# A two-layer hybrid decoder step: short head sums, fp32r norm sums, ordered weight parts and gating in two lines

## The chip, the cores and the metric

The kernel runs on one core of one Trainium2 chip. The metric is the device time of one execution, in microseconds (us); lower is better. Engines are named as the profile does: PE is TensorE's matmul, PEld its weight load, DVE is VectorE, ACT is ScalarE, POOL is GpSimd, SP is SyncE, which issues most transfers.

## The reference

One inference step of two layers, for a prompt of 256 rows and 8 sample rows that share all weights; D = 1024, feed-forward width 2816, everything in f32.

```python
def rmsnorm(x, g):
    y = x * lax.rsqrt(jnp.mean(x * x, axis=-1, keepdims=True) + EPS)
    return y * g
...
for i in range(DEPTH):                                     # 2
    x = x + 0.5 * swiglu(rmsnorm(x, norm_ffn1[i]), ...)
    h = rmsnorm(x, norm_mix[i])
    if i % 2 == 0:
        y, buf = short_conv_mixer(h, ...)                  # gated convolution of width 3
    else:
        y, S = hgrn2_mixer(h, rec_state, ...)              # 8 heads of 128, gated linear recurrence
    x = x + y
    x = x + cross_attn(rmsnorm(x, norm_xattn[i]), mem_k[i], mem_v[i], ...)   # 256 memory rows, 4 heads
    x = x + 0.5 * swiglu(rmsnorm(x, norm_ffn2[i]), ...)
y = rmsnorm(x, norm_final)
```

In the recurrent mixer the output of each head is `q` applied to the state, for the samples `o = (q*f) @ S0 + (q.k) v`; then

```python
o = rmsnorm(o, g_onorm) * silu(g)      # a norm over the 128 columns of each head
y = o.reshape(B, T, D) @ w_out
```

## The kernel before

The activations stay in SBUF, turned: `xT` holds 8 blocks (KT) of 128 columns of x on 128 partitions, with 264 columns (NC = 256 prompt rows + 8 samples). The weights stream through once. Each weight half (512 rows by 256 columns) is loaded (`raw`), rounded to fp32r on ScalarE (`wh`, L106) and its remainder computed on VectorE, in some stages on GpSimd (`wl`, L118). The activations are split the same way (`xh`, `xl`, L325 and L327). A product is then three fp32r matmuls, `wh*xh`, `wh*xl` and `wl*xh` (`mm3`, L303 to L305). Some smaller products are plain f32 matmuls, which show as two records each in the trace.

`project` runs a stage's chunks of 256 output columns. The first two chunks run together, staggered, in 16 groups of 6 matmuls, and hold all four PSUM banks for matmuls (`mm_bank`); the others follow one at a time. After a chunk half, `evac` reads the bank. It is issued under a raised priority, so the tile scheduler may put it ahead of other work of that engine.

All else is woven into the matmuls by `flow`. A `tick` (every 12 matmuls or so) advances the weights by one half (a split of `wl`, a rounding of `wh`, a load) and then takes one step of the front generator of each of three lanes. A generator that ends is taken out at the next step, and the next one of its lane comes up. The order in which the program issues things is not quite that in which an engine runs them: the scheduler fixes an order per engine by priority and its own estimate of what is ready, and the engines then run that order.

What the change and the prediction's steps touch:

- `Norm`: each block's square is added up on GpSimd (`nacc`, L336). After the last block, `finish` (lane 2) waits three steps, sums over partitions with an f32 matmul with `ones_d` (1/D everywhere, L345), and turns this into R, the reciprocal root: logarithm and exponential on ScalarE (L283), a Newton step on VectorE (L294, L298, L299). R multiplies the first bank of the next stage (L680 in the feed-forward, L814 in the attention, L741 and L743 in the convolution, L1046 in the recurrence). The first norm of the first layer is made in `start` instead.
- `out_proj`: the output projection of a mixer or an attention; `evac` adds the bank to `xT` (L722) and hands the block to the next norm.
- `attention`: `mem_split` (lane 1) rounds and splits the memory rows into `mh` and `ml` (L805, L806), one block per step; `do_kv` reads them after the queries' projection.
- `rec`: 16 chunks in the order f, q, f, q, i, i for heads 0 to 3 (group a = 0), the same for heads 4 to 7 (a = 1), then four chunks g. `chain(a)` (lane 0) makes the score matrices, `outputs(a)` (lane 1) the prompt's head outputs, `samples(a)` (lane 1) the samples': 16 matmuls per pair of heads with 32 columns of `qfz`, the product q*f (`pqs`, L1223), one copy of 512 columns to `os`, four transposes (`pqt`, L1238) and four additions that pick the diagonal (L1247). `head_norms(a)` (lane 2) squares the heads, sums over each head's 128 partitions with four matmuls with `strip` (`pm`, L1262) so that head hh's sum lies on partitions 32hh to 32hh+31, and makes `rs`, the reciprocal root. `gated(p)` (lane 2) spreads one row of `rs` over 128 partitions by a matmul with a column of the identity (`prs`, L1281), multiplies (L1285, L1286) and splits the result for the output projection (`yh` in the buffers `kg`, L1287; `yl` in `qf`, L1288). `before(k)` steps the flow until head k is made.

Lane 2 holds, in this order, `head_norms(0)`, `head_norms(1)`, `gated(0)` to `gated(3)`.

## Time and profile before

| | us |
|---|---|
| median of three runs | 1312.07 |
| lowest and highest | 1311.18, 1312.28 |
| profiled execution | 1312.63 |
| its span, first to last instruction | 1310.5 |

The profile is of one execution. Beside the page, these views are used: the waits (who waited for whom), the timeline (instructions of an engine in order of time: start, duration, engine, line, operation, tiles out<-in, forms and xcount; in brackets the idle time before one and what ended it), and the groups of instructions by line. Matmuls are pipelined, so their durations overlap; their cost is read from the distance between starts.

| engine | busy us | share of the span |
|---|---|---|
| PE | 1288.9 | 98% |
| DVE | 822.4 | 63% |
| ACT | 689.4 | 53% |
| POOL | 292.3 | 22% |

### The profile page before, as it was taken

The numbers are of one execution on the slowest core, as the hardware profiler recorded it, in microseconds if no ns is written. First come the engines' busy times: TensorE is split into PE (matmuls) and PEld (weight loads), VectorE is DVE, ScalarE is ACT, GpSimd is POOL, SyncE is SP. The second block draws the span as 40 slices with busy tenths as digits, with TensorE's granted clock in tenths as the row PEclk, the third lists the DMA queues.
The fourth block names the chain that finished last, engine by engine and source line by source line (L and its number), as shares of the span: only waits on it lengthen the run. The fifth ranks groups of instructions, "written<-read, shape, count | busy, mean of one in ns | idle before, by whom it ended". The sixth has DMA issues, their size and how long they took to land.

```text
span 1310.5 us, 25974 instructions
## 1 busy us (share of the span) xinstructions
PE 1288.9 (98%) x10330; PEld 1244.2 (95%) x10330; DVE 822.4 (63%) x1570; ACT 689.4 (53%) x1125; POOL 292.3 (22%) x236
## 2 busy tenths in 40 slices
PE   8999999999999999999999999999999999999997
PEld 7999999999869999999999999999999778999996
DVE  6655567759826655556555445878699637766454
ACT  6454544445545645544545544655665446666442
POOL 3211231212741111132111132000013521211220
PEclk9999999999999999999999999999999999999998
DMA  8796555646997666556666656554448995776650
GB/s 281 223 296 183 165 179 177 208 140 201 360 374 214 192 181 180 178 173 189 188 179 181 180 177 187 155 177 149 152 143 255 390 336 148 226 214 203 200 171 34
DMA packets 263099, 266.75 MB, mean 204 GB/s; under 512 B 8697, under 2 KB 259577, under 8 KB 260930
## 3 DMA queue, kind: packets, MB, share of 16 engines
q1 hardware_dynamic: 257150, 259.78, 63.8%
q10 hardware_dynamic: 5828, 5.32, 1.2%
q8 instruction: 81, 1.33, 0.4%
q14 instruction: 40, 0.33, 0.1%
HBM read 255.00 MB, written 10.07 MB: 202 GB/s over the span
## 4 chain that ended last, share of the span: by engine, by line
PE 92%; DVE 4%; ACT 2%; issue 1%; DMA 1%; POOL 0%; DVEq 0%; SPq 0%; ACTq 0%; POOLq 0%
PE pj L303 19%; PE pj L304 19%; PE pj L305 19%; PE dn L303 7%; PE dn L305 7%; PE dn L304 6%; PE kv L828 2%; PE kv L830 2%; PE kv L829 2%; DVE wl L118 1%; PE spv L984 1%; DVE xl L327 1%; PE psc L910 1%; PE pl L1139 1%; PE pj L370 1%; ACT wh L106 1%
## 5 line engine op out<-in xcount | busy, mean ns | idle before, releaser
L118 DVE TENSOR_TENSOR wl<-raw,wh 128x1024 fp32r<-128x1024 f32 (+1 forms) x347 | 425.4, 1230 | 247.4 <-ACT wh L106 232.3
L303 PE MATMUL pj<-xh,wh 128*128 128x264 f32 x1952 | 560.6, 287 | 2.0 <-DVE xT L722 2.0
L304 PE MATMUL pj<-xl,wh 128*128 128x264 f32 x1952 | 553.6, 284 | 0.0
L305 PE MATMUL pj<-xh,wl 128*128 128x264 f32 x1952 | 552.8, 283 | 0.0
L106 ACT CAST wh<-raw 128x1024 fp32r<-128x1024 f32 (+1 forms) x406 | 415.0, 1032 | 247.5 <-PE pj L304 123.7
L303 PEld LDWEIGHTS pj<-xh,wh 128*128 128x128 f32 x1952 | 367.7, 188 | 4.1 <-DVE xT L722 2.9
L304 PEld LDWEIGHTS pj<-xl,wh 128*128 128x128 f32 x1952 | 367.9, 189 | 0.3
L305 PEld LDWEIGHTS pj<-xh,wl 128*128 128x128 f32 x1952 | 366.2, 188 | 0.0
L303 PE MATMUL dn<-ah,wh 128*128 128x264 f32 x704 | 200.9, 285 | 0.0
L305 PE MATMUL dn<-ah,wl 128*128 128x264 f32 x704 | 200.0, 284 | 0.0
L304 PE MATMUL dn<-al,wh 128*128 128x264 f32 x704 | 199.4, 283 | 0.0
L118 POOL TENSOR_TENSOR wl<-raw,wh 128x1024 fp32r<-128x1024 f32 (+1 forms) x61 | 142.9, 2351 | 193.6 <-ACT wh L106 127.4
L688 POOL TENSOR_TENSOR al<-a,ah 128x264 fp32r<-128x264 f32 x88 | 90.2, 1027 | 418.3 <-ACT ah L687 418.2
L305 PEld LDWEIGHTS dn<-ah,wl 128*128 128x128 f32 x704 | 132.7, 188 | 0.0
L303 PEld LDWEIGHTS dn<-ah,wh 128*128 128x128 f32 x704 | 132.4, 188 | 0.2
L304 PEld LDWEIGHTS dn<-al,wh 128*128 128x128 f32 x704 | 132.5, 188 | 0.0
L283 ACT ACTIVATE g<-g 128x264 f32<-128x264 f32 x88 | 37.0, 424 | 81.3 <-DVE g L680 80.9
L687 ACT CAST ah<-a 128x264 fp32r<-128x264 f32 x88 | 36.0, 413 | 64.9 <-DVE a L686 64.4
L325 ACT ACTIVATE xh<-xT,gains 128x264 fp32r<-128x264 f32 x56 | 28.8, 514 | 77.2 <-DVE xT L714 59.2
L882 DVE CUSTOM_DVE_ANT_0 junk<-ring,pq 128x256 f32<-128x256 f32 x128 | 53.6, 419 | 3.7
L686 DVE TENSOR_TENSOR a<-g,pj 128x264 f32<-128x264 f32 x88 | 37.1, 426 | 28.7 <-PE pj L305 28.6
L680 DVE TENSOR_TENSOR g<-pj,R_norm_ffn 128x264 f32<-128x264 f32 x88 | 37.5, 429 | 27.4 <-PE pj L305 27.2
(321 smaller groups left out, 1497.8 us busy)
## 6 DMA issues: line engine op xcount, KB each, us to landing
raw<-in_w_ffn_gate_dram SPq DMA_DIRECT2D x88, 512.0 KB, 4.8
raw<-in_w_ffn_up_dram SPq DMA_DIRECT2D x88, 512.0 KB, 4.1
raw<-in_w_ffn_down_dram SPq DMA_DIRECT2D x64, 512.0 KB, 3.6
ring<-in_cache_mem_k_dram SPq DMA_DIRECT2D x16, 1024.0 KB, 8.5
raw<-in_w_xkv_dram SPq DMA_DIRECT2D x64, 256.0 KB, 3.8
ring<-in_cache_mem_v_dram SPq DMA_DIRECT2D x16, 1024.0 KB
raw<-in_w_rec_in_dram SPq DMA_DIRECT2D x32, 512.0 KB, 5.3
raw<-in_w_ffn_down_dram SPq DMA_DIRECT2D x32, 384.0 KB, 3.1
```

Source lines behind the costliest of these rows:

```text
L106: self.pin(copy(wh[:, :n], self.raw[i][:, :n]))
L118: self.pin(eng.tensor_sub(wl[:, :n], self.raw.pop(i)[:, :n], wh[:, :n].bitcast(F32)))
L283: in_line(nc.scalar.activation(dst, src, func, **kw))
L303: nc.tensor.matmul(ps, wh[:, s], rh, start=first, stop=False)
L304: nc.tensor.matmul(ps, wh[:, s], rl, start=False, stop=False)
L305: nc.tensor.matmul(ps, wl[:, s], rh, start=False, stop=last)
L325: pin(nc.scalar.activation(h, src, AF.Copy, scale=g))
L680: nc.vector.tensor_mul(g, ps, norm.R)
L686: nc.vector.tensor_mul(a, g, ps)
L687: nc.scalar.copy(ah[:, blk], a)
L688: nc.gpsimd.tensor_sub(al[:, blk], a, ah[:, blk].bitcast(F32))
L882: nc.vector.tensor_tensor_reduce(junk, t[:, i % 8], pq[:, :XD], 1.0, 0.0, ALU.mult, ALU.add, sc[:, h, i : i + 1])
```

## The change

1. Norm sums: `nacc` is split into a rounded part (ScalarE) and the remainder (VectorE) in the step in which the sum used to be issued, and two steps later two fp32r matmuls with an fp32r `ones_d` replace the f32 one. In steps: three waits, the split, two waits, the matmuls.
2. Head sums: four matmuls with a `mean` of 32 columns, each into its own 32 partitions, replace four accumulating ones with 128 columns.
3. `rs` is made fp32r: a copy rounds it, and one VectorE step leaves the rounded value on every partition but 1, 33, 65 and 97, where the remainder is kept (`seconds_of` is -1 there and 0 elsewhere). `pairs` adds a head's two rows in one fp32r matmul.
4. Samples: `qfz` holds the products on a diagonal of 4 by 4 for each half of the samples, so that matmuls with 4 columns accumulate a whole half of a head on 4 partitions; four strips for the four halves of a pair, four narrow copies, one transpose, one addition.
5. `gated(0)` and `gated(1)` go to lane 0; `made` becomes a set.
6. `mem_split` starts six steps later.
7. Weight parts: after the last sum of `out_proj` is issued and until the first two chunks of the next stage are, each `wl` on VectorE gets an ordering dependency (no semaphore) on that sum.

```diff
@@ Weights._split
-        self.pin(eng.tensor_sub(wl[:, :n], self.raw.pop(i)[:, :n], wh[:, :n].bitcast(F32)))
+        ins = eng.tensor_sub(wl[:, :n], self.raw.pop(i)[:, :n], wh[:, :n].bitcast(F32))
+        self.pin(ins)
+        if eng is nc.vector:
+            self.behind(ins)
@@ trunk_step
+    def order(ins, first, reason):
+        info = mybir.DependencyInfo(mybir.DependencyClass.NoSync, mybir.DependencyReason.DATA)
+        tc.add_manual_dep(ins.ins, first.name, info, reason=reason)
@@ Norm.finish
             yield
             yield
             yield
+            hi, lo = (cp.tile([P, NC], F32R, tag="nsq", name=n, bufs=2) for n in ("nhi", "nlo"))
+            nc.scalar.copy(hi, self.acc)
+            nc.vector.tensor_sub(lo, self.acc, hi.bitcast(F32))
+            yield
+            yield
             ps = aux_bank("ps_ms")
-            nc.tensor.matmul(ps[:, :NC], ones_d, self.acc, start=True, stop=True)
+            nc.tensor.matmul(ps[:, :NC], ones_d, hi, start=True, stop=False)
+            nc.tensor.matmul(ps[:, :NC], ones_d, lo, start=False, stop=True)
@@ project, after the first two chunks
             W.release()
+            W.behind = lambda ins: None
@@ prepare
+        nc.vector.tensor_add(pairs, ident[:, ::32], ident[:, 1::32])
+        nc.vector.reduce_sum(seconds_of, ident[:, 1::32], axis=AX.X)
+        nc.vector.tensor_scalar(seconds_of, seconds_of, -1.0, None, op0=ALU.mult)
@@ out_proj
-            nc.vector.tensor_add(xT[:, k], xT[:, k], ps)
+            add = nc.vector.tensor_add(xT[:, k], xT[:, k], ps)
+            if k == KT - 1:
+                W.behind = lambda ins: order(ins, add.ins, "the sum that frees a bank")
@@ attention, mem_split
+                for _ in range(6):
+                    yield
@@ rec
-            qfz = rp.tile([P, RH, 32], F32, name="qfz")
+            qfz = rp.tile([P, RH, 2, 16], F32, name="qfz")
+            os = rp.tile([P, P], F32, name="os")
+            nc.gpsimd.memset(os, 0.0)
...
-            nc.gpsimd.memset(strip[:, 3 * 32 : 4 * 32], 1.0 / P)
+            mean = rp.tile([P, 32], F32, name="mean")
+            nc.gpsimd.memset(mean, 1.0 / P)
@@ evac of a g chunk
                     if j == 1:
-                        flow.spawn(2, gated(p))
+                        flow.spawn(2 * a, gated(p))
@@ samples
-                    for hh in range(2):
-                        for hf in range(2):
-                            for j in range(4):
-                                nc.tensor.matmul(
-                                    ps[32 * j : 32 * j + 32, (2 * hh + hf) * P : (2 * hh + hf + 1) * P],
-                                    qfz[:, 2 * p + hh],
-                                    S0[:, hh, 4 * hf + j],
-                                    start=True,
-                                    stop=True,
-                                )
+                    for j in range(4):
+                        for c in range(4):
+                            hh, hf = divmod(c, 2)
+                            nc.tensor.matmul(
+                                ps[32 * c : 32 * c + 4, :P],
+                                qfz[:, 2 * p + hh, hf, 4 * j : 4 * j + 4],
+                                S0[:, hh, 4 * hf + j],
+                                start=j == 0,
+                                stop=j == 3,
+                            )
...
-                    os = tl("os", 1, (P, 4 * P))
-                    nc.scalar.copy(os, ps)
+                    for c in range(4):
+                        nc.scalar.copy(os[32 * c : 32 * c + 4], ps[32 * c : 32 * c + 4, :P])
...
-                    for i in range(4):
-                        nc.tensor.transpose(pt[:, i * P : i * P + P], os[:, i * P : i * P + P], ident)
+                    nc.tensor.transpose(pt[:, :P], os, ident)
@@ head_norms
-                    at = 32 * (GH - 1 - hh)
-                    nc.tensor.matmul(pm[:, :NC], strip[:, at : at + P], s["f"][:, hh], start=hh == 0, stop=hh == GH - 1)
+                    nc.tensor.matmul(pm[32 * hh : 32 * hh + 32, :NC], mean, s["f"][:, hh], start=True, stop=True)
...
-                newton(rs, pm[:, :NC], tmp)
+                newton(rr, pm[:, :NC], tmp)
+                nc.scalar.copy(rs, rr)
+                nc.vector.scalar_tensor_tensor(rs, rs.bitcast(F32), seconds_of, rr, op0=ALU.mult, op1=ALU.add)
@@ gated
-                        pr, ident[:, 32 * hh : 32 * hh + 1].broadcast_to([P, P]), s["rs"], start=True, stop=True
+                        pr, pairs[:, hh : hh + 1].broadcast_to([P, P]), s["rs"], start=True, stop=True
...
-                    made[0] = h + 1
+                    made.add(h)
@@ before
-                while made[0] <= k:
+                while k not in made:
```

## The prediction

> **What bounds the kernel now.** I read the page first: the busy shares, the granted clock and the chain that ended last.

> ```profile
> span 1310.5 us, 25974 instructions
> ...
> PE 1288.9 (98%) x10330; PEld 1244.2 (95%) x10330; DVE 822.4 (63%) x1570; ACT 689.4 (53%) x1125; POOL 292.3 (22%) x236
> ...
> PEclk9999999999999999999999999999999999999998
> ...
> PE 92%; DVE 4%; ACT 2%; issue 1%; DMA 1%; POOL 0%; DVEq 0%; SPq 0%; ACTq 0%; POOLq 0%
> ```

> TensorE is busy for 98% of the span at full clock, and 92% of the chain is its own. So a microsecond of matmul work taken out anywhere is a microsecond off the end, unless a wait grows into its place. The few per cent that belong to VectorE (DVE) are places where TensorE (PE) stands still. The view of waits, of PE alone, names those that the change can touch:

> ```profile
> PE pj L303 <- DVE xT L722: 2.0, 4, 1.0
> ...
> PE pj L303 <- ACT kg L1287: 0.3, 1, 0.3
> ```

> L722 is the sum in `out_proj` that frees a PSUM bank; it holds PE up four times (two mixers, two attentions). `kg` is the first gated head, under the buffer name that it reuses. I then went through PE's timeline around each operation that the diff rewrites, because durations of matmuls overlap: what a matmul costs is the distance between the starts of its neighbours.

> **The norm sums (ones_d).** A sum of the second layer's first norm, in PE's timeline:

> ```profile
> 624.08 0.28 PE L304 MATMUL pj<-xl,wh 128*128 128x264 f32 x1
> 624.20 0.28 PE L305 MATMUL pj<-xh,wl 128*128 128x264 f32 x1
> 624.32 0.61 PE L345 MATMUL ps_ms<-nacc_norm_ffn,ones_d 128*128 128x264 f32 x2
> 624.57 0.48 PE L303 MATMUL pj<-xh,wh 128*128 128x264 f32 x1
> 624.89 0.29 PE L304 MATMUL pj<-xl,wh 128*128 128x264 f32 x1
> ```

> An fp32r matmul over 264 columns starts 0.12 after its neighbour. The f32 sum is two passes (x2): from 624.20 to 624.89 is 0.69; less the two fp32r matmuls in it (0.24) it costs 0.45. The change puts two fp32r matmuls there, 0.24. Seven norms go through `finish` (the first of the eight does not): 7 x 0.21 = 1.5 us gained.

> **Spreading the head norms (prs).** In the same view, at the end of the recurrent layer's projection:

> ```profile
> 947.38 0.28 PE L305 MATMUL pj<-xh,wl 128*128 128x264 f32 x1
> 947.50 0.61 PE L1281 MATMUL prs<-rs,ident 128*128 128x264 f32 x2
> 947.75 0.48 PE L303 MATMUL pj<-xh,wh 128*128 128x264 f32 x1
> 948.06 0.28 PE L304 MATMUL pj<-xl,wh 128*128 128x264 f32 x1
> ```

> From 947.38 to 948.06 is 0.68, less 0.24: 0.44. After the change the rounded value and its remainder lie on two partitions of `rs`, and one fp32r matmul with `pairs` adds them: 0.12. Eight heads: 8 x 0.32 = 2.6 us.

> **The head norms' sums (pm).** Four f32 matmuls into one accumulator become four with 32 columns each, into four separate strips of the array:

> ```profile
> 944.15 0.28 PE L305 MATMUL pj<-xh,wl 128*128 128x264 f32 x1
> 944.27 1.94 PE L1262 MATMUL pm<-f,strip 128*128 128x264 f32 x8
> 945.85 0.48 PE L303 MATMUL pj<-xh,wh 128*128 128x264 f32 x1
> 946.17 0.28 PE L304 MATMUL pj<-xl,wh 128*128 128x264 f32 x1
> ```

> Now they take 2.02 less 0.24, 1.78. The nearest row for the new form is `pqs`, which already uses four strips:

> ```profile
> 853.48 0.28 PE L305 MATMUL pj<-xh,wl 128*128 128x264 f32 x1
> 853.69 1.08 PE L1223 MATMUL pqs<-ring,qfz 128*32 128x128 f32 x32
> 854.70 0.39 PE L303 MATMUL pj<-xh,wh 128*128 128x264 f32 x1
> 854.93 0.28 PE L304 MATMUL pj<-xl,wh 128*128 128x264 f32 x1
> ```

> Its 32 passes take 1.45 less 0.24, 1.21. One pass over 128 columns is 0.11 (the transposes below), so 32 passes four abreast are 0.88, and 0.33 goes into entering and leaving the strips. For `pm`: 8 passes four abreast are two of 0.22, 0.44, and with 0.33 that is 0.77. Gain 2 x (1.78 - 0.77) = 2.0 us. The ends: nothing if the strips don't run abreast, 2 x (1.78 - 0.44) = 2.7 if entering and leaving cost nothing here; I stay with the row that has the same form.

> [...]

> **The samples.** The 16 matmuls of a pair stay 16, again over four strips, but now accumulate four to a strip: no change by the row above. Three of four transposes go:

> ```profile
> 857.16 0.60 PE L1238 MATMUL pqt<-ident,os 128*128 128x128 f32 x4
> 857.59 0.29 PE L1240 MATMUL pd<-qk,ones 128*128 128x16 f32 x2
> ```

> Four take 0.43, one 0.11; 4 pairs x 3 x 0.11 = 1.3 us. Twelve small additions leave VectorE; ScalarE gets four narrow copies for one wide one. The nearest narrow copy:

> ```profile
> L991 ACT COPY os<-spv 8x256 f32<-8x256 f32 x4 | 1.5, 364 | 1.3 <-PE spv L984 1.3
> ```

> So at most 1.5 us of ScalarE per pair; the transpose comes a whole flow step later and ScalarE is half idle, so I cost it at nothing. If that cover failed, PE would wait under 1 us per pair.

> PE work so far: 1.5 + 2.6 + 2.0 + 1.3 = 7.4 us.

> **The ordered weight parts.** The longest of the four bank waits, VectorE first and then PE:

> ```profile
> 305.73 1.21 DVE L118 TENSOR_TENSOR wl<-raw,wh 128x1024 fp32r<-128x1024 f32 x1
> 306.86 0.41 DVE L722 TENSOR_TENSOR xT<-xT,pj 128x264 f32<-128x264 f32 x1
> ```
> ```profile
> 306.06 0.29 PE L305 MATMUL pj<-xh,wl 128*128 128x264 f32 x1
> 307.33 0.39 PE L303 MATMUL pj<-xh,wh 128*128 128x264 f32 x1 [0.99 <-DVE xT L722]
> 307.56 0.28 PE L304 MATMUL pj<-xl,wh 128*128 128x264 f32 x1
> ```

> A weight split of the next stage stands in front of the last sum. Counting the splits in order, this is the fourth half of the stage that follows, which the program issues after the sum; the three other places have the same fourth half in front. The new dependency forbids just this. With the sum at 305.73 it ends at 306.14, before PE needs the bank (306.06 + 0.12). Here an idle of 0.99 costs 1.27 - 0.12 = 1.15 between the starts, and restarting 0.1 more (307.33 to 307.56): 0.26 besides the idle. All four idle 2.0 in the view of waits, so 2.0 + 4 x 0.26 = 3.0 us is what can go; I take 2.4, since a sum that comes in time by 0.04 will not always do so, and 1.2 as the low end. What is queued behind the sum now is that split (1.21), then the splits after it. PE uses it only in the second half of the weights, over 5 us later, so nobody waits.

> The later memory splits help the same queue. In the first attention they stand in front of the norm:

> ```profile
> 309.64 2.85 DVE L806 SCALAR_TENSOR_TENSOR ml<-memT,gains,mh 128x256 fp32r<-128x256 f32 x7
> 312.42 0.42 DVE L294 SCALAR_TENSOR_TENSOR nacc_norm_xattn<-ps_ms,R_norm_xattn 128x264 f32<-128x264 f32 x1
> ```

> They go six steps back and end two steps before their first reader's stage (16 steps lie in between, they need 14). They then meet the sample scores on VectorE, which is also nearly full; a split at 0.41 per step is less than a step of 12 matmuls (1.45), so I cost it at nothing, with 0.5 us per attention if VectorE falls behind.

> **Gating in its own line.** The first four heads no longer queue behind the second group's norm. Per head VectorE has the first row below, the second, and a product of the same 264 columns (0.43, the rows after them): 1.3 us.

> ```profile
> L1285 DVE SCALAR_TENSOR_TENSOR oT<-oT,gon,prs 128x264 f32<-128x264 f32 x8 | 3.7, 483 | 0.0
> L1288 DVE TENSOR_TENSOR qf<-oT,kg 128x264 fp32r<-128x264 f32 x8 | 3.4, 429 | 0.8 <-ACT kg L1287 0.8
> ```
> ```profile
> 935.99 0.43 DVE L1090 TENSOR_TENSOR G<-pj,R_norm_mix 128x264 f32<-128x264 f32 x1 [3.86 <-PE pj L305]
> 937.37 0.43 DVE L1093 TENSOR_TENSOR q<-q,G 128x264 f32<-128x264 f32 x1 [0.95 <-ACT q L283]
> 939.97 1.23 DVE L118 TENSOR_TENSOR wl<-raw,wh 128x1024 fp32r<-128x1024 f32 x1 [2.17 <-ACT wh L106]
> ```

> Idle in this gap, while the `g` chunks are projected: 3.86 + 0.95 + 2.17 = 7.0 us, for 4 x 1.3 = 5.2. What goes is PE's 0.3 for `kg` and its restart, 0.26: 0.6. The ends are 0, if the second group's heads make PE wait as the first do now, and 1.2, if a second stop goes that the view of waits is too coarse to name. New there: a copy and a subtract to split `rs`, 0.36 and 0.48 by the quoted rows, 0.9 us later per group with the handover; the second group's first head is due 8 x 6 x 0.12 = 5.8 us into the output projection, which covers it.

> **The later norm sums.** This is the part that can cost. The sum's matmul moves two flow steps, 24 matmuls or 2.9 us. In the stage of the first fence:

> ```profile
> 626.87 0.43 DVE L299 SCALAR_TENSOR_TENSOR R_norm_ffn<-nacc_norm_ffn,R_norm_ffn 128x264 f32<-128x264 f32 x1
> ...
> 631.12 0.80 DVE L680 TENSOR_TENSOR g<-pj,R_norm_ffn 128x264 f32<-128x264 f32 x2 [0.46 <-PE pj L305]
> ```

> R is ready at 627.30 and first read at 631.12: 3.8 us to spare, of which 2.9 go and 0.2 come back by the shorter sum. About 1.1 is left, and PE needs the bank that this multiply frees only 9 matmuls (1.1) after filling it, of which the multiply takes 0.43: some 0.6 more. The copy and the subtract that split the sum run before that, on idle engines. In the attentions less is spare, but the memory splits in front are gone. I take 0.5 us over all seven (ends 0 and 3).

> **Sum.** 7.4 + 2.4 + 0.6 - 0.5 = 9.9 us. The profiled execution took 1312.63 (span 1310.5, 2.1 around it): 1302.7. It lay 0.6 above the median of the three runs, 1312.07, so on the median's scale 1302.2.

> **Rivals.** *The order changes nothing* (the change doesn't do what it says): if the split in front of the sum were issued before it, or if another VectorE instruction took its place, the bank waits stay. For it: VectorE has no gap around 306. Against: the count of halves. Time: 1302.2 + 2.4 = 1304.6. Chance 0.13.

> *PE waits in line for the second group's `rs`.* The first `prs` of that group is issued one step after `pm`, 1.45 us, while `rs` goes the way of R, 3.0 us from the sum's start (624.32 to 627.30 in the rows above), and 0.9 for its split: 3.9 - 1.45 = 2.5 us of idle PE, 1304.7. Against it: there are fp32r matmuls enough to stand in front of it, the rest of the last `g` chunk and 5.8 us of the output projection. Chance 0.07. [...]

> *Slower: R comes late.* If weight splits slip between the steps of the norm on VectorE, R misses the first bank. One split of 1.21 is covered by 1.1 + 0.6; each further one stalls PE by about 1.2 in each of seven stages. Without R's 0.5 the change gains 10.4; that and the 2.6 us below which nothing can be told are 13.0, 1.9 per stage. So it decides from three splits in a row, 3 x 1.21 - 1.7 = 1.93: 7 x 1.93 = 13.5, 1312.07 - 10.4 + 13.5 = 1315.2. For it: in the first attention seven memory splits did stand in front of the norm. Against: the row at 631.12 shows VectorE waiting for PE. Chance 0.03.

> **How the numbers follow.** Forecast 0.73, rivals 0.13, 0.07 and 0.03; 0.04 for several small losses together that end within 0.2% of before (2.6 us, about what a measurement of this kernel can tell from no change). The best end of every term, 7.4 + 0.7 + 3.0 + 1.2 = 12.3, gives 1299.8. Of the bad ends, `pm` not abreast, the low end of the bank waits, nothing from gating and 1 us for R make 5.4 + 1.2 - 1 = 5.6, 1306.5, and hold both middle rivals. Range 1299.5 to 1306.5. Faster are the forecast and those two, with 0.01 of the small losses: 0.94; same 0.03, slower 0.03.

> **What would show it.** In the new profile: `ps_ms` at 0.24 per norm, `prs` at 0.12 and from about 930 on, `pm` under 0.8, one transpose per pair; no wait of PE for the sum of `out_proj`, and the fourth split behind it; the first multiply by R still waiting for PE and not for VectorE. Wrong would be new PE waits behind R, `rs` or `mh`, or a busy PE that shrinks by 7 us while the span does not.

## The result and the profile after

The changed kernel takes 1303.21 us, the median of four runs (1303.12 to 1303.39), against 1311.62 us for the kernel before (four runs, 1310.90 to 1312.28). The ratio is 0.9936, with a 95% interval of 0.9919 to 0.9953: faster, by 8.4 us. The forecast was 1302.2. The profiled executions are 1303.28 (span 1301.3) and, before, 1312.63 (span 1310.5).

One caution about these numbers: in the profiled run of before the granted clock was 0.50 for 3.4 us near the start (12.7 to 16.1 us), too little to change a digit of PEclk on the page, and the run of after does not show this. A second profile of the kernel before (`control`, below) doesn't have it either, and its span is 1309.0. So the change itself is worth 7.7 us of span, and the rest of the 9.2 between the first two profiles is that start; probably the rest of the 8.4 between the medians is too.

The page of after, with the rows that stood first in the prediction:

```profile
span 1301.3 us, 25953 instructions
...
PE 1279.6 (98%) x10310; PEld 1236.4 (95%) x10310; DVE 824.1 (63%) x1570; ACT 694.5 (53%) x1146; POOL 293.5 (23%) x236
...
PE 94%; DVE 3%; ACT 2%; issue 0%; DMA 0%; POOL 0%; DVEq 0%; SPq 0%; ACTq 0%; POOLq 0%
```

PE still bounds the kernel, and its share of the chain that ended last grew from 92% to 94%. Busy time of PE fell by 9.3 us, as much as the span (both with the start of before in it). The waits of PE in the kernel after (line waited for, total us, times, longest):

```profile
PE pj L308 <- DVE qT L833: 2.3, 2, 1.2
...
PE pj L308 <- ACT kg L1308: 1.3, 1, 1.3
```

The four waits for the sum of `out_proj` are gone, as forecast. Two kinds have come in: PE now waits in each attention for the queries scaled by R (L833), and once, longer than the 0.3 of before, for the first gated head of the second group (`kg`, L1308).

PE's timeline in after, at the four places whose matmuls were rewritten (start, duration, line, tiles, xcount):

```profile
308.92 0.28 PE L310 MATMUL pj<-xh,wl 128*128 128x264 f32 x1
309.04 0.28 PE L355 MATMUL ps_ms<-nhi,ones_d 128*128 128x264 f32 x1
309.16 0.28 PE L356 MATMUL ps_ms<-nlo,ones_d 128*128 128x264 f32 x1
309.28 0.28 PE L308 MATMUL pj<-xh,wh 128*128 128x264 f32 x1
...
854.01 0.27 PE L1261 MATMUL pqt<-ident,os 128*128 128x128 f32 x1
854.12 0.29 PE L1263 MATMUL pd<-qk,ones 128*128 128x16 f32 x2
...
938.97 0.28 PE L310 MATMUL pj<-xh,wl 128*128 128x264 f32 x1
939.18 0.65 PE L1281 MATMUL pm<-f,mean 128*32 128x264 f32 x8
939.77 0.39 PE L308 MATMUL pj<-xh,wh 128*128 128x264 f32 x1
939.99 0.28 PE L309 MATMUL pj<-xl,wh 128*128 128x264 f32 x1
...
948.03 0.28 PE L309 MATMUL pj<-qf,wh 128*128 128x264 f32 x1
948.41 0.72 PE L1302 MATMUL prs<-rs,pairs 128*128 128x264 f32 x4
948.97 0.28 PE L310 MATMUL pj<-kg,wl 128*128 128x264 f32 x1
```

The norm sum takes 0.24 (308.92 to 309.28, less one pitch of 0.12), the transpose 0.11, `pm` 938.97 to 939.99 less 0.24, so 0.78, and four `prs` 948.41 to 948.97, so 0.14 each. The forecast had 0.24, 0.11, 0.77 and 0.12. `pm` starts 0.21 after its neighbour and the matmul behind it gives way after 0.22; `pqs` in before has 0.21 and 0.23 at the same places (853.48 to 853.69, 854.70 to 854.93), against the 0.12 between other neighbours.

To see where the time went I compare when the n-th projection matmul starts in two traces; the difference is the lead. Against `control`, whose start is like that of after, the lead grows like this:

| stretch | forecast | lead gained, us |
|---|---|---|
| seven norm sums, 0.18 each (read where one stands alone) | 1.5 | 1.3 |
| recurrent layer: `pm` twice 1.0, `pqt` four times 0.33, `prs` 2.6 | 5.9 | 5.9 |
| recurrent layer: stops around the gated heads | +0.6 | -0.7 |
| feed-forwards behind the attentions, less their sums: bank wait gone | 1.2 (half of 2.4) | 0.5 + 0.8 = 1.3 |
| attentions, less their sums: bank wait gone, R late | 1.2 - 0.5 | -0.1 - 0.1 |
| start | - | 0.1 |
| all (rounded terms add up to 7.7) | 9.9 | 7.6 |

`prs` in this table is 8 x (0.44 - 0.12), with 0.12 for the four that stand alone in after; the recurrent stops are what is left of the 5.2 us gained in that layer, and the rest are differences of the lead. The matmul work, 7.2 of 7.4, came as forecast. The waits did not: the forecast had them better by 2.5 and they are better by 0.4.

The attention's new stop, in VectorE's, ScalarE's and PE's timelines of after:

```profile
310.81 2.35 DVE L119 TENSOR_TENSOR wl<-raw,wh 128x1024 fp32r<-128x1024 f32 x2
313.08 0.43 DVE L299 SCALAR_TENSOR_TENSOR nacc_norm_xattn<-ps_ms,R_norm_xattn 128x264 f32<-128x264 f32 x1
...
314.01 0.43 DVE L304 SCALAR_TENSOR_TENSOR R_norm_xattn<-nacc_norm_xattn,R_norm_xattn 128x264 f32<-128x264 f32 x1
314.55 1.11 DVE L833 TENSOR_TENSOR qT<-pj,R_norm_xattn 128x264 f32<-128x264 f32 x3
```
```profile
309.06 1.99 ACT L107 CAST wh<-raw 128x1024 fp32r<-128x1024 f32 x2
310.95 0.47 ACT L288 ACTIVATE R_norm_xattn<-ps_ms,eps_t 128x264 f32<-128x264 f32 x1
311.45 0.42 ACT L288 ACTIVATE R_norm_xattn<-R_norm_xattn 128x264 f32<-128x264 f32 x1
```
```profile
313.53 0.28 PE L310 MATMUL pj<-xh,wl 128*128 128x264 f32 x1
315.04 0.39 PE L308 MATMUL pj<-xh,wh 128*128 128x264 f32 x1 [1.23 <-DVE qT L833]
```

The sum's matmuls ran at 309.04 and 309.16, but the logarithm waits on ScalarE behind two weight roundings until 310.95, and the Newton steps on VectorE behind a weight split until 313.08, although the exponential ended at 311.87. PE has the bank back at 315.04 in the place of 313.65: 1.39 lost here, and 1.25 in the second attention. The wait for the sum of `out_proj`, 1.15 earlier in the same stage, is gone; the two cancel.

### The profile page after: what moved, and what is told of

The parts are those of the page before. It is cut to its first block, busy times and chain, and to the rows that moved or that the text cites. A ratio compares the mean times of both kernels' runs of the same rounds, so it can differ in the third digit from the quotient of the medians.

```text
span 1301.3 us, 25953 instructions
## 1 busy us (share of the span) xinstructions
PE 1279.6 (98%) x10310; PEld 1236.4 (95%) x10310; DVE 824.1 (63%) x1570; ACT 694.5 (53%) x1146; POOL 293.5 (23%) x236
## 3 DMA queue, kind: packets, MB, share of 16 engines
q8 instruction: 81, 1.33, 0.4%
## 4 chain that ended last, share of the span: by engine, by line
PE 94%; DVE 3%; ACT 2%; issue 0%; DMA 0%; POOL 0%; DVEq 0%; SPq 0%; ACTq 0%; POOLq 0%
PE pj L308 20%; PE pj L309 19%; PE pj L310 19%; PE dn L308 7%; PE dn L310 7%; PE dn L309 7%; PE kv L847 2%; PE kv L849 2%; PE kv L848 2%; PE spv L1003 1%; PE psc L929 1%; PE pl L1163 1%; DVE wl L119 1%; PE pj L381 1%; DVE xl L332 1%; ACT wh L107 1%
```

## The experiments

Times are medians; "undone" and "more" mean against the changed kernel, 1303.21. The runs were made in three rounds on three chips; the kernel before, run beside each, took 1311.61 to 1311.92, so 0.3 us lies between the rounds. Where a median moves by less than 1 us, the stretch from the 1301st projection matmul to the last is given too, which leaves the start out: 1118.2 in after, 1125.7 in `control`.

**no_order**: the ordered weight parts undone.

```diff
             add = nc.vector.tensor_add(xT[:, k], xT[:, k], ps)
-            if k == KT - 1:
-                W.behind = lambda ins: order(ins, add.ins, "the sum that frees a bank")
```

> The changed kernel without the ordering of the weight parts. Theory (VectorE sets the pace in the attentions): the bank waits return at all four joints, about 2.0 us idle in all. At the two joints into a feed-forward they cost 0.5 us each. At the two joints into an attention they cost nearly nothing, because TensorE, 1.2 and 0.9 us later there, then waits that much less for R, which VectorE delivers at the same time as before. Total 1.0 to 1.5 us slower than the changed kernel (1303.2): 1304.5. Rival (each wait adds by itself): 3.0 us slower, 1306.2. Second rival (the order does nothing): 1303.2.

Measured 1304.37 (1304.26 to 1305.82), 1.2 more; the stretch is 0.65 longer. The waits of PE show why it isn't 3:

```profile
PE pj L308 <- DVE xT L737: 1.6, 4, 1.0
```

The four bank waits are back, and the wait for the queries has left the list: where the bank comes late, R has time to arrive. Each attention can lose its time once, at either place. By the lead, the order saves 0.5 and 0.8 us in the two feed-forwards and gives 0.1 and 0.5 of that back in the two attentions; the rest of the 1.2 comes behind the last projection. The theory holds, the forecast's 2.4 does not.

**sum_early**: the two further steps ahead of the norm sums taken out.

```diff
             nc.vector.tensor_sub(lo, self.acc, hi.bitcast(F32))
-            yield
-            yield
             ps = aux_bank("ps_ms")
```

> The changed kernel with the two extra steps before the norm sums taken out again: split and sum are issued in one step. Theory (R comes late in the attentions because the Newton steps stand behind splits on VectorE): they now stand in front of two of the weight splits, so the waits of TensorE for the first multiply by R (1.2 and 1.1 us) go: 2.3 to 2.6 us faster than the changed kernel, 1300.8. Rival (the two steps were needed): TensorE waits at the sum itself for its two parts, 0.3 to 1.0 us in each of seven norms, and the kernel is the same or up to 4 us slower.

Measured 1307.42 (1307.21 to 1308.93), 4.2 more; the theory fell and the rival holds. The waits for the queries did leave PE's list, but PE has lost more by then. PE and VectorE in the first attention's norm:

```profile
306.51 0.28 PE L310 MATMUL pj<-xh,wl 128*128 128x264 f32 x1
307.28 0.39 PE L355 MATMUL ps_ms<-nhi,ones_d 128*128 128x264 f32 x1 [0.49 <-ACT nhi L350]
308.27 0.39 PE L356 MATMUL ps_ms<-nlo,ones_d 128*128 128x264 f32 x1 [0.60 <-DVE nlo L351]
```
```profile
306.10 1.78 DVE L119 TENSOR_TENSOR wl<-raw,wh 128x1024 fp32r<-128x1024 f32 x1
307.80 0.42 DVE L351 TENSOR_TENSOR nlo<-nacc_norm_xattn,nhi 128x264 fp32r<-128x264 f32 x1
```

The matmul for the rounded part waits for a copy on ScalarE, that for the remainder for a subtraction that stands behind a weight split; 1.76 go between 306.51 and 308.27, where 0.24 would do. The projection matmuls behind them do not need the sum, yet the next one starts only at 308.50. The two steps that I had booked as a cost of 0.5 are what the split sum needs to be free.

**ml_behind**: the low parts of the memory ordered behind R's last Newton step.

```diff
-                    nc.vector.scalar_tensor_tensor(
+                    low = nc.vector.scalar_tensor_tensor(
                         ml[:, k], memT[:, k], g, mh[:, k].bitcast(F32), op0=ALU.mult, op1=ALU.subtract
                     )
+                    order(low, norm.last.ins, "the norm first")
```

(`norm.last` is the last Newton step of the norm.)

> The changed kernel, in which the VectorE part of each memory split also gets an ordering dependency on the last Newton step of the norm. Theory (eight memory splits, 3.2 us on VectorE, are what makes R late in the attentions, since six steps later in the program did not move them behind the norm): R comes 1 to 2 us earlier, the two waits for R go, 2.0 to 2.6 us faster than the changed kernel, 1301.0. Rival (the later sum makes R late): no change, 1303.2, with the Newton steps as late as they were. Second rival: the splits, pushed back, make the keys and values wait: slower by up to 2 us.

Measured 1311.40 (1309.87 to 1313.21), 8.2 more: it loses the whole gain. VectorE around R, then PE at the scores of the first attention:

```profile
313.26 0.43 DVE L304 SCALAR_TENSOR_TENSOR R_norm_xattn<-nacc_norm_xattn,R_norm_xattn 128x264 f32<-128x264 f32 x1
313.61 1.27 DVE L825 SCALAR_TENSOR_TENSOR ml<-memT,gains,mh 128x256 fp32r<-128x256 f32 x3
314.80 1.45 DVE L834 TENSOR_TENSOR qT<-pj,R_norm_xattn 128x264 f32<-128x264 f32 x4
```
```profile
360.88 0.38 PE L981 MATMUL pst<-ident,tops 4*128 4x4 f32 x2 [1.16 <-DVE tops L979]
```

R's last step starts 0.75 earlier (313.26 against 314.01), but three of the parts that were pushed back slip in ahead of the queries, and the stop gets longer. The other five then stand among the sample scores, and PE waits at the top scores, 46 us later. By 421 us 2.9 us are lost, and 5 more in the second attention. Of those 5, 1.5 are not waiting. PE stands still for 1.91 us ahead of 985.52, and then the granted clock falls (busy times of PE, PEld, DVE, ACT, POOL, then the granted clock, DMA share and GB/s):

```profile
982.23:985.64 3.41, 1.50 (x13) 1.29 (x12) 3.34 (x9) 1.05 (x1) 0.00 (x0) 1.00 0.73 231
985.64:989.05 3.41, 3.41 (x16) 3.41 (x17) 3.25 (x6) 1.45 (x3) 0.00 (x0) 0.50 0.32 99
989.05:992.46 3.41, 3.41 (x30) 3.41 (x29) 2.65 (x11) 0.94 (x2) 0.00 (x0) 1.00 0.87 274
```

For 3.41 us PE runs 16 matmuls where it otherwise runs 30. The only one of the ten executions whose mean clock was 0.998 took 1309.87, 6.7 more. So the order itself costs about 6.5, and the clock the rest. The theory (1301.0) fell. That what is pushed back is late further on was foreseen in direction; the place, VectorE's scores, and the size were not.

**rs_f32**: the head norms kept in f32, spread by a column of the identity as before.

```diff
-                newton(rr, pm[:, :NC], tmp)
-                nc.scalar.copy(rs, rr)
-                nc.vector.scalar_tensor_tensor(rs, rs.bitcast(F32), seconds_of, rr, op0=ALU.mult, op1=ALU.add)
+                newton(rs, pm[:, :NC], tmp)
...
-                        pr, pairs[:, hh : hh + 1].broadcast_to([P, P]), s["rs"], start=True, stop=True
+                        pr, ident[:, 32 * hh : 32 * hh + 1].broadcast_to([P, P]), s["rs"], start=True, stop=True
```

> The changed kernel with rs left in f32 and spread by f32 matmuls with a column of the identity, as before the change; all else as changed. Theory (the split of rs is what makes the second group late): rs of the second group is ready about 2.5 us earlier, the wait of TensorE for the gated head (1.3 us idle, 1.5 with the restart) and for prs (0.2) go, and eight spreads cost 0.32 more each, 2.6: net 0.9 slower, 1304.1. Rival (the wait has another cause, VectorE or the order of the lanes): it stays, 2.6 us slower, 1305.8.

Measured 1304.52 (1304.17 to 1304.87), 1.3 more; the stretch is 0.8 longer. PE has 2.6 us more to do, and its wait for `kg` is gone: with the short matmuls PE comes to `kg` sooner, and the copy and the subtraction that make `rs` two fp32r rows bring `kg` later; half of what the short matmuls save goes into that wait.

**control**: the kernel before, profiled again.

> The kernel before, unchanged, profiled a second time, for one question: in the profiled run of before the granted clock fell to 0.68 and 0.50 between 12 and 16 us, and the 100th projection matmul started at 26.00 us, against 24.15 us after the change. If that slow phase belongs to the kernel before, the 100th matmul starts again near 26.0 us and the span is about 1310.5 us; then 1.8 us of the measured gain come from the start. If it belongs to that one execution, the matmul starts near 24.2 us here, and the span of this run is about 1308.7 us; then the gain of the two profiled runs overstates that of the change by 1.8 us.

Measured 1310.93, span 1309.0; the 101st projection matmul starts at 24.27 against 26.00 in the first profile of before. The busy times by stretch, columns as above, first of before, then of `control`:

```profile
12.00:14.00 2.00, 1.91 (x11) 1.66 (x10) 2.00 (x6) 2.00 (x4) 2.00 (x2) 0.68 1.10 350
14.00:16.00 2.00, 2.00 (x11) 2.00 (x11) 2.00 (x7) 2.00 (x4) 2.00 (x2) 0.50 1.09 342
```
```profile
12.00:14.00 2.00, 1.92 (x15) 1.70 (x14) 2.00 (x7) 2.00 (x4) 2.00 (x2) 1.00 1.09 348
14.00:16.00 2.00, 2.00 (x18) 2.00 (x18) 2.00 (x7) 2.00 (x4) 2.00 (x1) 1.00 1.09 347
```

In each of these windows before ran 11 matmuls, at a clock of 0.68 and 0.50, where `control` ran 15 and 18 at 1.00. The phase belongs to the execution, not to the kernel.

**lane2**: the gating of the first four heads back in lane 2.

```diff
-                        flow.spawn(2 * a, gated(p))
+                        flow.spawn(2, gated(p))
```

> The changed kernel with one part undone: the gating of the first four heads is put back in the third lane, behind the chain of the second group's work. The forecast counted this part at 0.6 us, with ends at 0 and 1.2: by that, 1303.8 us, between 1303.2 and 1304.4. A rival says that the part is worth more: with all eight heads gated at the end, VectorE has some 1.7 us of work for each of four more heads ahead of what the output projection needs first, and TensorE stands still for 3 us or more: 1306 us or above. Told apart by where TensorE's stop at the output projection stands and how long it is.

Measured 1306.45 (1306.13 to 1307.26), 3.2 more; the rival holds. PE at the start of the output projection:

```profile
942.62 0.52 PE L1302 MATMUL prs<-rs,pairs 128*128 128x264 f32 x3
944.71 0.76 PE L308 MATMUL pj<-kg,wh 128*128 128x264 f32 x4 [1.57 <-ACT kg L1308]
...
946.96 0.48 PE L1302 MATMUL prs<-rs,pairs 128*128 128x264 f32 x2 [0.41 <-DVE rs L1288]
```

One long stop and several short ones follow each other, with all eight heads to be gated on VectorE while PE has only the output projection. In before, with its longer matmuls, the same lane costs less (1.1 us, under `order_only`); that PE was late enough there to hide the rest fits, but is not shown by itself.

**rs_order**: the rounding copy on VectorE, weight parts ordered behind the rounded difference.

```diff
-                nc.scalar.copy(rs, rr)
-                nc.vector.scalar_tensor_tensor(rs, rs.bitcast(F32), seconds_of, rr, op0=ALU.mult, op1=ALU.add)
+                nc.vector.tensor_copy(rs, rr)
+                split = nc.vector.scalar_tensor_tensor(rs, rs.bitcast(F32), seconds_of, rr, op0=ALU.mult, op1=ALU.add)
+                if a: W.behind = lambda ins: order(ins, split.ins, "the head norms first")
```

> The changed kernel, with VectorE in the place of ScalarE for the copy that rounds the head norms, and with the low weight parts that are split from then on ordered behind the second group's rounded difference. In the changed kernel TensorE stands still for 1.49 us more than a matmul's pitch ahead of the first output projection matmul that takes the gated second group. Theory: that stop is the head norms being late, because the copy (0.43 us, behind a sigmoid and a table load on ScalarE) and a weight part of 1.2 us on VectorE stand ahead; both taken away, the stop goes and the time is 1301.7 us. Rival: the weight part that is pushed back is then the late one, TensorE waits for it in the place of the gated heads, and the time stays within 0.4 us of 1303.2 us.

Measured 1303.09 (1302.93 to 1304.09), the same within the measurement; the profiled run had the low clock at its start, and its stretch is 0.2 shorter. The stop at `kg` went from 1.33 to

```profile
951.05 0.39 PE L308 MATMUL pj<-kg,wh 128*128 128x264 f32 x1 [0.60 <-ACT kg L1309]
```

and no new wait for a weight part appeared, so the cause named is right for half of the stop; 0.56 is lost again in the second attention, where R comes later. On the clock the theory (1301.7) was not reached.

**qt_first**: in the attentions, weight parts held until the first four query tiles are scaled.

```diff
-        self.W.advance()
+        if not self.hold: self.W.advance()
...
-            newton(self.R, ps[:, :NC], self.acc)
+            newton(self.R, ps[:, :NC], self.acc); flow.hold = self.name == "norm_xattn"
...
-                nc.vector.tensor_mul(qTs[h][:, j], ps, norm.R)
+                q = nc.vector.tensor_mul(qTs[h][:, j], ps, norm.R)
+                if (h, j) == (1, 1): W.behind = lambda ins: order(ins, q.ins, "the queries first")
```

(The hold ends after those four are issued.)

> The changed kernel, where in both cross-attentions the weight parts that come up while R of the norm is made are held until the first four query tiles have been scaled by R. Theory: in the changed kernel TensorE stops for 1.39 and 1.25 us more than a matmul's pitch because R comes late, and R is late by one weight part of 1.22 us on VectorE that runs between R's exponential and its Newton steps; with that part behind, each stop shrinks by 1.1 to 1.2 us, and the time is 1300.9 us. Rival: as with the memory splits that were ordered behind R, the work that is pushed back is late further on (the scores of the samples, the K and V projections), and the time is 1303 us or more.

Measured 1311.37 (1311.13 to 1312.57), 8.2 more. At its own place the theory is right: the Newton steps start at 311.86 instead of 313.08, and at 321 us the kernel leads after by 1.2 us. Then it loses 4.6 by 377 us. In the second attention it gains 0.6 and loses 4.7, and 0.6 more goes behind the last projection. The waits of PE in this kernel that after doesn't have:

```profile
PE pst L981 <- DVE tops L979: 2.6, 2, 1.3
PE spv L1004 <- DVE Ps L991: 2.1, 2, 1.0
PE ppt L944 <- DVE Pp L922: 1.9, 2, 0.9
```

All three are VectorE's part of the scores. In the changed kernel VectorE is nearly full there (busy 14.13 of 15):

```profile
315.00:330.00 15.00, 14.96 (x113) 14.45 (x114) 14.13 (x47) 6.28 (x8) 3.24 (x2) 1.00 0.76 240
```

What is pushed behind R lands in a stretch that has no room, and it comes back as several stops. The rival holds, and it explains the waits of `ml_behind` in the same way.

**order_only**: the kernel before with only the parts that move work (the order, lane `2 * a` with `made` as a set, the six steps ahead of the memory splits).

> The kernel before with the parts of the change that only move work: weight parts ordered behind the last sum of an output projection, the gating of the first four heads in a lane of its own, the memory splits six steps later. Every matmul is as before. Theory: these parts are worth what undoing them cost in the changed kernel, 1.2 us for the order and 3.2 us for the gating's lane, so 1311.6 less 4.4: 1307.2 us. Rival, the forecast's sizes: 2.4 and 0.6, so 1308.6 us. Second rival: the early gating of four heads only pays where the matmuls that carry the head norms are short, since each of the four is 0.32 us longer here and stands in the middle of the projection: 1309.5 us or more.

Measured 1308.41 (1308.27 to 1310.08), ratio to before 0.9978 (0.9968 to 0.9987): 3.3 faster. The theory's 4.4 fell; the first rival, the forecast's sizes, was right to 0.2 us in the sum. By the lead against `control` the order is worth 2.0 here (2.4 in the forecast) and the lane 1.1 (0.6), so part of that closeness is luck.

**work_only**: the changed kernel with all short matmuls, and none of the parts that move work (`no_order`, `sum_early`, `lane2` and `mem_now` in one).

> The counterpart: the changed kernel with all its shorter matmuls, but every part that moves work undone: no order for the weight parts, gating in the third lane, norm sums without the two further steps, memory splits without their six steps. Theory, the parts add up: 1303.2 and 1.2 and 3.2 and 4.2 make 1311.8 us, so that the shorter matmuls alone give nothing at all, although they take some 7 us off TensorE. Rival: the stops overlap (the late R covers the wait for a bank, and the stop at the gated heads covers what is lost earlier), and 1308 us or less is seen.

Measured 1312.49 (1311.62 to 1313.89), ratio to before 1.0004 (0.9995 to 1.0014): no gain at all. The losses add up, as the theory had it. The waits that eat the 7 us:

```profile
PE pj L308 <- DVE xT L737: 1.9, 4, 1.0
PE pj L308 <- ACT kg L1308: 1.6, 1, 1.6
PE ps_ms L356 <- DVE nlo L351: 1.5, 2, 1.0
```

Besides these it has the many short stops seen in `lane2` and `sum_early`. Of the 9.3 us above the changed kernel, 4.2 by `sum_early` belong to the two steps ahead of the norm sums, which only a split sum needs. So this is not the short matmuls at their best: with the two steps kept, they alone should be worth some 3 to 4 us. That is an estimate from these runs; the kernel was not run.

**mem_now**: the six steps ahead of the memory splits taken out.

```diff
-                for _ in range(6):
-                    yield
```

> The changed kernel without the six steps ahead of the memory splits. The forecast costed this part at nothing: 1303.2 us within 0.4. In the changed kernel's trace the eight splits run ahead of R's Newton steps with the six steps too. Rival: without them three of the splits get ahead of the rounded difference of the norm sum on VectorE, the sum's matmul then waits for it and R comes later by some 1.2 us in each attention: 1305 us.

Measured 1304.28 (1303.64 to 1305.09). The mean clock of all four executions is 0.996, and in the profiled one the granted clock fell near the start and cost 1.2 us, which is about all of the difference. Its stretch is 0.6 shorter than in after, because the second attention's stop shrinks (the two stops for the queries are 1.7 together instead of 2.3). By the stretch it is no loss; whether the later start is good for anything is left open. What is plain is that it doesn't do what I said: in after the eight splits still run from 307.64 to 310.89, ahead of R. The six steps only put three of them behind the norm sum's rounded difference (`nlo`) where `mem_now` has them in front of it, and this did not make R later, so the rival fell. Presumably the scheduler takes ready work forward.

**mem_rs**: `mem_now` and `rs_order` together.

> Both of these: memory splits without the six steps, and the head norms' copy on VectorE with the weight parts ordered behind their rounded difference, which took the stop ahead of the gated second group from 1.49 to 0.76 us. If the memory splits' place is worth nothing, 1302.5 us; if it helps R, 1302 us or less; by its rival, 1304 us.

Measured 1302.65 (1302.32 to 1303.76), ratio to before 0.9934 (0.9919 to 0.9949), stretch 0.9 shorter than in after. It is the fastest kernel of the study, by 0.6 us over the changed one: less than a measurement of this kernel can tell.

## Why the prediction was right, and where it was not

*PE's work, 7.4 us.* Right: 7.2, and each of the four prices within 0.02 us per instruction or 0.03 per sum. The price of `pm`, taken from `pqs` with an estimate of 0.33 for entering and leaving the strips, came out at 0.78 for 0.77; without the 0.33 the forecast would have been 0.44.

*That this work comes off the end.* Right for the change as a whole, but for a reason that I had not seen. "A microsecond of matmul work taken out anywhere is a microsecond off the end, unless a wait grows into its place": `work_only` shows waits growing into all of it, 0 gained. The parts that I booked as small, 2.4 and 0.6 and -0.5, are what lets the 7 us through. The moves alone give 3.3, the short matmuls alone 0, and both 8.4. Of the 5.1 missing in that sum, 4.2 is what the two steps save by `sum_early`, which only the split norm sum needs; the rest is that the order and the lane are worth more or less with what stands beside them.

*Ordered weight parts, 2.4 (ends 1.2 and 3.0).* The mechanism is right: all four waits for the sum went. The term came out at 1.3, near the low end (0.65 when it alone is undone, 2.0 among the matmuls of before), for a reason other than the one given: in both attentions the next wait was R, 1.39 and 1.25 late, where I had expected none. I asked who waits for the split that is pushed back, but not what the freed 1.15 us exposes next.

*The later norm sums, -0.5.* I worked the slack out in a feed-forward, where it was right (no wait for R there), and applied it to the attentions, on the word that "the memory splits in front are gone". They are not gone: on VectorE the six steps move only three of the eight, and none past R. And ScalarE's two roundings in front of the logarithm (1.9 us) were not in the working at all. The sign of the term was wrong as well in another sense: without the two steps the kernel is 4.2 slower.

*Gating in its own line, +0.6 (ends 0 and 1.2).* In the sum it came out at -0.7: the stops around the gated heads grew. The step that failed is that the cover of 5.8 us is enough for the second group's first head. The cover is there, but `rs` is ready 9.1 us after `pm` (939.18, to 948.26, the end of the difference), not 3.9. On the first part of the way a table load (1.28, from 940.29) stands ahead of the logarithm, a weight rounding (1.04) ahead of the exponential and a weight split (1.23) ahead of the Newton steps. The last part, in VectorE's and ScalarE's timelines of after:

```profile
945.32 0.43 DVE L304 SCALAR_TENSOR_TENSOR rr<-G,rr 128x264 f32<-128x264 f32 x1
...
947.77 0.49 DVE L1288 SCALAR_TENSOR_TENSOR rs<-rs,seconds_of,rr 128x264 fp32r<-128x264 f32 x1 [0.47 <-ACT rs L1287]
```
```profile
945.59 0.42 ACT L288 ACTIVATE q<-G 128x264 f32<-128x264 f32 x1
946.03 1.28 ACT L284 ACT_TABLE_LOAD   x1
947.33 0.41 ACT L1287 CAST rs<-rr 128x264 fp32r<-128x264 f32 x1
```

The Newton step is done at 945.75; the copy that rounds it waits on ScalarE for a sigmoid and for the load of another activation table (1.28) until 947.33. Yet undoing this part costs 3.2: its worth depends on the short matmuls.

*Rivals.* "PE waits in line for the second group's `rs`" happened in small: 0.11 idle at `prs` and 1.33 at `kg`, of 2.5 forecast. "R comes late" happened in two of seven stages by one split each, far from the three in a row from which it decides. "The order changes nothing" is refuted by `no_order`.

*The time.* 1303.2 for 1302.2. The forecast started from an execution that had lost 1.5 us to a low clock at its start; set against `control`, the change is worth 7.6 of the 9.9 forecast by the lead. The miss is in the waits, the hit in the work, and that the time came within 1.0 us is in part luck: the medians differ by 0.8 more than that lead.

What is not settled: why the clock falls after some stretches with few matmuls and not after others (see the end), and what the rest of the stop at `kg` (0.60 in `rs_order`) waits for in turn.

## What to carry to other kernels

Where one engine is 98% busy, work taken from it counts only as far as the engines that feed it keep up at those very places; price the next wait behind each one that is removed, by the stage's own queue on every engine in the chain (here ScalarE's two roundings as well as VectorE's split). When a matmul is split in two so that its operands must first be rounded, issue it later by as much as the rounding takes, because the queue behind it stood while it waited (in `sum_early` 1.76 us went where 0.24 would do). Work that is pushed out of a tight place has to land where its engine has room: both tries to free R put it into a stretch that was 94% full, and cost 8.2 us in `qt_first` and, without its loss of clock, some 6.5 in `ml_behind`, some two and a half to three times the 2.6 that the late R takes.

## What the runs showed of the hardware

Apart from the end of the execution (from 1303.0 of 1310.5 us in before, from 1294.1 of 1301.3 in after, when PE has started its last matmul), the granted clock fell in 5 of the 14 profiled executions: near the start in before, `rs_order`, `mem_now` and `work_only`, where it cost 1.0 to 1.7 us, and at 985.64 us in `ml_behind`, where it cost 1.5. The length of the wait ahead did not decide in these runs. In before the clock fell after PE had stood still for 1.26 us near 3.8 and 1.47 near 10.3 us (transfers not yet landed, then the first weights not yet rounded), in `control` it stayed at 1.00 after 1.06 at the second of these places, and in after it stayed after 1.05 and 0.74. But in `sum_early` it stayed at 1.00 after 1.16 and 1.27, and in `rs_order` it fell after 1.03 and 1.26.

In after a change between two sets of activation functions cost ScalarE no more than the load itself, 1.28 us: a sigmoid ends at 946.01, the load runs from 946.03 to 947.31, and the next copy starts at 947.33.
